# A hybrid DeltaNet/Mamba layer: the first gate blocks between the last tokens' norms, the stream's sums ahead of the taps, the second gate pair in eight products

## The chip, the cores and the metric

The kernel runs on one core of a Trainium2 chip. The metric is the device time of one execution in microseconds (us), the median of several runs. A core has TensorE (PE, matrix products), VectorE (DVE), ScalarE (ACT), GpSimd (POOL) and SyncE (SP), whose queue issues most of the transfers; each works through its own list of instructions in order and waits for the others by semaphores. Tiles lie in SBUF; products are accumulated in the banks of PSUM, 128 partitions of 512 float32 values each.

## The reference, cut to what matters

One layer over 1024 latent tokens (a grid of 16 rows of 64) with a prefix of 256 context tokens, width 1024, all float32. The token mixers (a gated DeltaNet and a Mamba-2 scan, side by side) are not touched by the change; it lies between their output and the feed-forward.

```python
mod = silu(c) @ w_ada + b_ada                       # (6 * 1024,)
sh1, sc1, g1, sh2, sc2, g2 = split(mod, 6)
...
x = x + g1 * (mix_x @ w_out)                        # 1024 x 1024
h = rmsnorm(x, norm2_g) * (1 + sc2) + sh2
a = dwconv2d_grid(h @ w_gate, conv_w, conv_b)       # 3x3 depthwise over the 16 x 64 grid
x = x + g2 * ((silu(a) * (h @ w_up)) @ w_down)      # w_gate, w_up: 1024 x 2816, w_down: 2816 x 1024
return rmsnorm(x, final_norm_g)
```

## The kernel before

**Tiling.** Tokens go in eight tiles of 128 (called tokens 0 to 7 below, `t` in the code). A float32 product is made of three matmuls in a shorter format: each operand is split into a high part (a cast, names in `h`) and a low part (what is left, names in `l`), and high by high, high by low and low by high are summed in PSUM. One matmul is 128x128 by 128x512. The 2816 columns of the feed-forward are 22 blocks of 128, taken as 11 pairs (`FORD` lists them; a pair is block j and block j + 11).

**Order.** The instructions of each engine are put in order by a scheduler of the language, which starts from the order of the code and runs its own estimate of the time; the code steers it by where a call stands, by the number of buffers of a tile, and by explicit dependences. The order shown further down is its result.

**From the output projection to the norm.** The loop over `half` and `c` makes the output projection (L1350) for four tokens and 512 columns at a time: 24 matmuls into one bank, then a multiplication by the gate row and an addition of the residual into `x1[t]`. The last round is the second half of the tokens (4 to 7) with `c` = 0. When a token has both halves of its columns, `norm2(t)` runs: a square with a sum on ScalarE, a scale and shift of that sum (L104 helper), a power on POOL (L1292), two wide operations on `u` (the second, the shift, is on POOL for tokens 0 to 3 and on VectorE from 4 on, `SHD`), eight transposes on TensorE (L1323), and out of PSUM the high part `mxh` (cast, L1325) and the low part `mxl` (L95 helper). These two hold the stream h, transposed, until the end of the feed-forward. Meanwhile the adaLN rows `aac` are summed up on POOL (L98) and spread over the partitions by TensorE (L689). `x1` goes to DRAM (`x_d`, L1327).

**First gate pair.** Only after the loop are the PSUM pools of the mixers closed and that of the feed-forward (`ps2`) opened: two images of 1024 columns (two banks each, tag `img`) and four single banks (`pb`). `first_gate` loads and splits the weights `gh`, `gl` of two blocks, and `fmm` (L1301) makes their images, 24 matmuls for each half of the tokens, 96 in all.

**Stream sums, taps, first up pair.** From the second pair on, a pair is made by a form with seven block products rather than eight (`group7`, L1459): the four weight blocks are combined by sums on POOL, the stream by sums T1 to T4 (`tq`, loop over `u`: four additions of high and low part and four subtractions on VectorE, then casts L1594 and low parts), and the products are combined by VectorE as they leave PSUM (`combine`; the first, P1, is copied by ScalarE at L1536). One product is 12 matmuls, a pair 84. `conv` takes an image: the centre tap on ScalarE writes `fac`, eight more taps on VectorE (L107) add to it, ScalarE makes the SiLU; the taps are queued in `todo` and handed out by `pop`. The up blocks of the first pair are plain products (96 matmuls, `fmm`), copied to SBUF by ScalarE and multiplied with `fac` later.

**Steady loop and end.** The products then alternate: gate pair 1, gate pair 2, up pair 1, gate pair 3, up pair 2, and so on (`seq7`; pairs count from 0). `prepare` runs four products ahead, and a pair's weights are loaded (`raw`, L1429) when its first product is prepared. Finished pairs are combined again for a seven-product form of the down projection (`asums`: stores to `sa_d`, L1509; `wsums` for `w_down`: stores to `sw_d`, L1498), which comes last (L1717), with the reload of `x1` (L1753) for the residual and the final norm.

In the names, a number behind a letter group is only the buffer's (`fac11` excepted: there it is the block).

Of the kernel before, what the change touches and what calls it, by code (L numbers as in the profile page):

```python
# [18 lines left out]
P = 128  # L19
# [54 lines left out]
def hybrid_layer(ctx: ExitStack, tc: tile.TileContext, x, c, cx, c_ctx, w_ada, b_ada, norm1_g, w_in,  # L74
# [1206 lines left out]
    rot = dict(ob="BXA")  # L1281
# [22 lines left out]
    with pool("op") as op:  # L1304
        lp["op"] = op
        for n_, shape, dt, b_ in (("n2g", [P, 512], F32, 1), ("abi", [1, 512], F32, 1), ("aac", [P, 512], F32, 2),
                                  ("awa", [P, 2, 512], F32, AWB), ("xr", [P, D], F32, XRB), ("u", [P, D], F32, 2)):
            T(op, shape, "res_" + n_, dt, tag=n_, bufs=b_)
        for j, n_ in ((2, "sc2row"), (1, "sh2row")):
            rows[j] = T(op, [P, D], n_)  # L1310
        for n_, dt, b_ in (("owr", F32, 2), ("owh", F32R, OWB), ("owl", F32R, OWB)):
            T(op, [P, 512], "res_" + n_, dt, tag=n_, bufs=b_)

        def norm2(t):
# [4 lines left out]
            for i in range(2):  # L1319
                pb = bank("ip")  # L1320
# [12 lines left out]
        for half in range(2):  # L1333
            for c in ((0, 1), (1, 0))[half]:
                if not (half and c):
                    if half + c == 0:
                        wout(0, 0, ws, KO[W0N:], (0,) * 8)
                    else:
                        ws = {}
                        wout(c, half, ws, KO, WHERE[half])  # L1340
                for t in range(4 * half, 4 * half + 4):
# [3 lines left out]
                    pb = rbank("ob")  # L1345
# [16 lines left out]
                    if c == 1 - half:  # L1362
                        norm2(t)
        rows[3] = T(tka[0], [P, D], "g2row", tag="grow")
        for b in (6, 7):
            ada_put(op, bank("tp"), b, late_ac[b])


        def first_gate(f):
            ws = []  # L1370
            for i in range(2):
                raw = T(op, [P, 512], f"gr{f}{i}", tag="owr", bufs=2)
                nc.sync.dma_start(raw.rearrange("p (k m) -> p k m", m=P),
                                  w_gate[512 * i:512 * i + 512, f * P:(f + 1) * P].rearrange("(k p) m -> p k m", p=P))
                wh = T(op, [P, 512], f"gh{f}{i}", F32R, tag="owh", bufs=OWB)
                wl = T(op, [P, 512], f"gl{f}{i}", F32R, tag="owl", bufs=OWB)
                nc.scalar.copy(wh, raw)
                tt(wl, raw, wh.bitcast(F32), ALU.subtract)
                ws.append([w.rearrange("p (k m) -> p k m", m=P) for w in (wh, wl)])
            return [lambda k, j=j: ws[k // 4][j][:, k % 4, :] for j in range(2)]  # L1380


        pspx.__exit__(None, None, None)
        ps2 = ctx.enter_context(pool("ps2", space=PSUM))

        def image():
            cnt[0] += 1
# [476 lines left out]
```

## Time and profile before

| | us |
|---|---|
| median of 3 runs | 1562.47 |
| lowest and highest | 1554.84, 1564.5 |
| the profiled execution | 1562.9 |
| its span | 1561.1 |

The profile is of one execution; its clock starts with the span. "Busy" counts work and not waiting, and a row of the timeline gives start, length, engine, line, operation, tiles (written tile, arrow, read tiles), shape and count, and in brackets how long the engine had been idle and what released it. L92, L95, L98, L104 and L107 are one-line helpers for ScalarE, VectorE and POOL operations, so the tiles' names say which of their uses a row is. The mean granted clock of TensorE in the profiled execution is 0.961 of full speed.

The page in shares of the span:

| engine | busy us | share |
|---|---|---|
| PE | 1417.2 | 91% |
| DVE | 1174.8 | 75% |
| ACT | 738.5 | 47% |
| POOL | 809.8 | 52% |

### The profile page before, as it was taken

Reading aid. Unit: us, or ns where it says so; the run is one execution under the profiler, and the core shown is the slowest. Engines: PE = TensorE matmul, PEld = TensorE weight load, DVE = VectorE, ACT = ScalarE, POOL = GpSimd, SP = SyncE. Lnnn points to the kernel's source line nnn. Section 1 sums busy time; section 2 is a strip of 40 time slices with the busy share of each in tenths; the row PEclk is TensorE's granted clock in tenths of the full one; section 3 lists DMA queues with packets and bytes.
Section 4 is the critical chain, followed back from the end, with each engine's and each line's share of the span. In section 5 each row is a group of like instructions: output and inputs, shape, how many; then the busy total and the mean of one; then the engine's idle time right before and its main releaser. Section 6 shows DMA issues by size and latency. Waiting matters only on the chain. (4 is left out here: it accounts for less than half of the span.)

```text
span 1561.1 us, 24442 instructions
## 1 busy us (share of the span) xinstructions
PE 1417.2 (91%) x8104; PEld 1172.1 (75%) x8104; DVE 1174.8 (75%) x1875; ACT 738.5 (47%) x1655; POOL 809.8 (52%) x797
## 2 busy tenths in 40 slices
PE   5899888999999889998995948999999998999997
PEld 2577776777888789997774736877787787788786
DVE  5877688977536666547987679989999999557686
ACT  6566645636666656455243243333333333365553
POOL 3554499782125775301474278687888888200001
PEclk8999999999999999999997979999999999999999
DMA  7454777654668685444962024344444444996732
GB/s 262 131 148 138 235 214 216 172 151 113 184 188 300 193 254 182 139 126 161 323 217 81 24 78 162 109 148 155 154 157 151 146 154 166 342 322 212 228 108 108
DMA packets 269308, 275.14 MB, mean 176 GB/s; under 512 B 51936, under 2 KB 194909, under 8 KB 269183
## 3 DMA queue, kind: packets, MB, share of 16 engines
q1 hardware_dynamic: 259935, 244.10, 49.6%
q0 software_dynamic: 7904, 26.74, 4.6%
q10 hardware_dynamic: 1344, 2.75, 0.5%
q8 instruction: 64, 1.05, 0.3%
q14 instruction: 61, 0.50, 0.1%
HBM read 196.06 MB, written 77.46 MB: 175 GB/s over the span
## 5 line engine op out<-in xcount | busy, mean ns | idle before, releaser
L1439 ACT CAST wh<-rw 128x512 fp32r<-128x512 f32 x282 | 165.7, 620 | 289.5 <-POOL rw L98 92.9
L98 POOL TENSOR_TENSOR wl<-rw,wh 128x512 fp32r<-128x512 f32 x144 | 199.5, 1405 | 86.5 <-ACT wh L1439 83.7
L107 DVE SCALAR_TENSOR_TENSOR fac<-im,v,fac 128x945 f32<-128x945 f32 (+2 forms) x176 | 209.6, 1209 | 29.6 <-ACT fac L92 26.8
L1459 PE MATMUL pb<-mxh,wh 128*128 128x512 f32 x320 | 128.9, 403 | 37.0 <-ACT wh L1439 17.8
L1459 PE MATMUL pb<-tq,wh 128*128 128x512 f32 x480 | 147.0, 390 | 1.8 <-ACT wh L1439 1.8
L95 DVE TENSOR_TENSOR wl<-rw,wh 128x512 fp32r<-128x512 f32 x138 | 92.1, 702 | 56.3 <-ACT wh L1439 56.2
L455 PE MATMUL bk<-hh,wh 128*128 128x512 f32 x320 | 129.6, 406 | 0.7 <-DVE v L256 0.7
L455 PE MATMUL bk<-hh,wl 128*128 128x512 f32 x320 | 129.5, 405 | 0.0
L1459 PE MATMUL pb<-mxl,wh 128*128 128x512 f32 x320 | 127.5, 398 | 1.8 <-POOL mxl L98 1.8
L455 PE MATMUL bk<-hl,wh 128*128 128x512 f32 x320 | 128.6, 402 | 0.0
L1459 PE MATMUL pb<-mxh,wl 128*128 128x512 f32 x320 | 127.0, 397 | 0.0
L98 POOL TENSOR_TENSOR rw<-rw,rw 128x512 f32<-128x512 f32 x80 | 111.5, 1406 | 13.3 <-DMA rw<-in_ffn_w_up_dram 6.4
L1787 POOL TENSOR_TENSOR ss<-ss,mhalf 128x1 f32<-128x1 f32 x8 | 7.3, 920 | 198.0 <-DVE ss L95 198.0
L1459 PEld LDWEIGHTS pb<-tq,wh 128*128 128x128 f32 x480 | 90.4, 188 | 21.5 <-ACT wh L1439 2.5
L1459 PEld LDWEIGHTS pb<-mxh,wh 128*128 128x128 f32 x320 | 61.9, 193 | 53.7 <-ACT wh L1439 18.2
L1459 PE MATMUL pb<-tq,wl 128*128 128x512 f32 x240 | 92.0, 390 | 0.7 <-POOL wl L98 0.7
L1459 PEld LDWEIGHTS pb<-mxl,wh 128*128 128x128 f32 x320 | 62.1, 194 | 14.9 <-POOL mxl L98 2.2
L1459 PEld LDWEIGHTS pb<-mxh,wl 128*128 128x128 f32 x320 | 61.8, 193 | 13.2
L455 PEld LDWEIGHTS bk<-hh,wh 128*128 128x128 f32 x320 | 61.7, 193 | 13.3 <-PE bk L254 0.9
L455 PEld LDWEIGHTS bk<-hh,wl 128*128 128x128 f32 x320 | 61.7, 193 | 13.1 <-issue 0.9
L455 PEld LDWEIGHTS bk<-hl,wh 128*128 128x128 f32 x320 | 61.7, 193 | 12.1 <-issue 0.2
L95 DVE TENSOR_TENSOR rw<-rw,rw 128x512 f32<-128x512 f32 x56 | 68.3, 1241 | 0.5 <-DMA rw<-in_ffn_w_down_dram 0.2
(415 smaller groups left out, 4160.8 us busy)
## 6 DMA issues: line engine op xcount, KB each, us to landing
rw<-in_ffn_w_down_dram SPq DMA_DIRECT2D x77, 256.0 KB
rw<-sa_d SPq DMA_DIRECT2D x77, 256.0 KB
kv<-kv_d SPq DMA_DIRECT2D x80, 192.0 KB
yq<-yq_d SPq DMA_DIRECT2D x64, 192.0 KB
awa<-in_w_ada_dram SPq DMA_DIRECT2D x24, 512.0 KB
rw<-in_ffn_w_up_dram SPq DMA_DIRECT2D x44, 256.0 KB
sa_d<-fac SPq DMA_DIRECT2D x44, 256.0 KB
sw_d<-rw SPq DMA_DIRECT2D x44, 256.0 KB
```

The lines of the kernel that those rows point to most:

```text
L95: nc.vector.tensor_tensor(o, a, b, op=op)
L98: nc.gpsimd.tensor_tensor(o, a, b, op=op)
L107: nc.vector.scalar_tensor_tensor(o, a, s, b, op0=op0, op1=op1)
L455: paced(nc.tensor.matmul(pb[:, :bn], w[i][:, kk, :], hview(h, k, b0, bn), start=(n == 0), stop=(n == 3 * KT - 1)))
L1439: nc.scalar.copy(h, r)
L1459: nc.tensor.matmul(pv, w[:, q], m[:, :, k, :], start=(n == 0), stop=(n == 11))
L1787: nc.gpsimd.tensor_tensor(rs, rs, mhalf[:, 0:1], op=ALU.pow)
```

## The change

1. The feed-forward's PSUM pool is opened before the products of the last four tokens, and these and their transposes use its four single banks. `early_gate` puts gate work between them: at token 5 the weights of the first gate pair are loaded and split, at tokens 5 and 6 the low token halves of the two images are written, at token 7 both high halves. The adaLN rows 6 and 7 go through the same banks.
2. In the feed-forward's set-up the first up block's weights are cast before the centre taps of the first pair. The stream's sums are now a function; sums 0 and 1 stand ahead of the first pair's taps (the first tap waits in VectorE's order behind their last subtraction), sums 2 and 3 behind the up products.
3. The second gate pair is made of plain products (96 matmuls) straight into its images, without weight sums and without combining. The first pair's up products are multiplied ahead of it.
4. A pair's weights are loaded seven products ahead, not four; the taps are handed out in other numbers per product; the first `wsums` comes with the first up pair of the loop.
5. `x1` is reloaded by one call for each block of the second down product, not in a loop of its own.
6. The pool of `sm` is laid before that of `fac`, `aac` moves behind `sc2row` and `sh2row`, and the banks of the output products rotate over another set.

```diff
-    rot = dict(ob="BXA")
+    rot = dict(ob="BXE")
...
+        def early_gate(t):
+
+            if t == 5:
+                first_im.extend(image() for f in FORD[:2])
+                fw0.extend(first_gate(f) for f in FORD[:2])
+            if t in (5, 6):
+                fmm(first_im[t - 5][:, LOH], *fw0[t - 5], 0)
+            if t == 7:
+                for b in range(2):
+                    fmm(first_im[b][:, HIH], *fw0[b], 512)
...
-                pb = bank("ip")
+                pb = pp["pb"]() if pp else bank("ip")
...
+                if half and not c:
+                    pspx.__exit__(None, None, None)
+                    ps2 = ctx.enter_context(pool("ps2", space=PSUM))
+                    pp["pb"] = pbank
...
-                    pb = rbank("ob")
+                    pb = pp["pb"]() if pp else rbank("ob")
...
+                    if half and not c:
+                        early_gate(t)
...
-        for i in range(2):
-            for b in range(2):
-                fmm(first_im[b][:, HB[i]], *fw0[b], 512 * i)
...
-    def conv(f, im, ac):
+    def conv(f, im, ac, behind=None):
...
+        if behind is not None:
+            tc.add_manual_dep(ctr.ins, behind.ins.name, NOSYNC, reason="first up columns first")
...
+            if behind is not None and i == 0:
+                tc.add_manual_dep(x_.ins, hist["sub"].ins.name, NOSYNC, reason="sums of the stream first")
...
+    parts = {("u", 0): [split(w) for w in wplain["u", 0]]}
+    first_cast = hist["cast"]
...
-    for u in range(4):
+    def tsums(u):
...
+    tsums(0)
+    tsums(1)
     for b in range(2):
         acs[0, b] = fac(FORD[b])
-        conv(FORD[b], im0[b], acs[0, b])
-    groups = {("g", 1): group7(w_gate, FORD[2], FORD[3])}
+        conv(FORD[b], first_im[b], acs[0, b], first_cast)
...
+    tsums(2)
+    tsums(3)
+    for b in (1, 0):
+        wplain["g", b] = wload(w_gate, FORD[2 + b])
+    for i, r in enumerate(up0):
+        o = acs[0, i // 2][:, HB[i % 2]]
+        tt(o, r, o, ALU.mult)
+    for b in (1, 0):
+        parts["g", b] = [split(w) for w in wplain["g", b]]
+        im = image()
+        plain("g", b, parts["g", b], [im[:, q] for q in HB])
+        acs[1, b] = fac(FORD[2 + b])
+        conv(FORD[2 + b], im, acs[1, b])
+    groups = {("g", 2): group7(w_gate, FORD[4], FORD[5])}
+    asums(0, acs.pop((0, 0)), acs.pop((0, 1)))
...
-    for j in range(1, NP + 1):
+    for j in range(2, NP + 1):
...
-    AHEAD = 4
+    AHEAD, LOADS7 = 4, 7
...
-        pop(2 if n in (3, 6) or j == NP - 1 else 1)
+        pop((2, 2, 2 if k == "u" else 1, 0 if k == "u" else 1, 1, 1, 1)[n])
+        if (k, j, n) == ("u", 1, 3):
+            wsums(0)
...
+            if p == "P4" and j < NLC:
+                nc.gpsimd.dma_start(x1[j], x1_d[j])
```

**The order on TensorE around the last four tokens.** Of the kernel before: the last matmul of token 7's output product (written to a bank `bk`; `owh` is the high part of `w_out`), the spreading of an adaLN row, and the transposes of `u3` to `u5`, the normalised tokens 3 to 5.

```order
L1350 MATMUL bk468_9582<-owh013_9434,mxl_8507 128x512
L689 MATMUL bk471_9631<-aac6_9103,ones_69 128x512
L1323 MATMUL bk453_9259<-ident_64,u3_9253 128x128 x4
L1323 MATMUL bk454_9266<-ident_64,u3_9253 128x128 x4
L689 MATMUL bk472_9634<-aac7_9178,ones_69 128x512
L1323 MATMUL bk460_9471<-ident_64,u4_9465 128x128 x4
L1323 MATMUL bk461_9478<-ident_64,u4_9465 128x128 x4
L1323 MATMUL bk463_9519<-ident_64,u5_9513 128x128 x4
L1323 MATMUL bk464_9526<-ident_64,u5_9513 128x128 x4
```

All four products stood ahead of the transposes of tokens 3 to 7. Of the changed kernel, the end of token 5's product (bank `pb462`), the transposes of token 5 and the start of token 6's product (`pb467`):

```order
L1394 MATMUL pb462_9490<-owh013_9434,mxh_8506 128x512
L1394 MATMUL pb462_9490<-owl013_9435,mxh_8506 128x512
L1394 MATMUL pb462_9490<-owh013_9434,mxl_8507 128x512
L1363 MATMUL pb463_9523<-ident_64,u5_9517 128x128 x4
L1363 MATMUL pb464_9530<-ident_64,u5_9517 128x128 x4
L1394 MATMUL pb467_9588<-owh010_9392,mxh_8506 128x512
L1394 MATMUL pb467_9588<-owl010_9393,mxh_8506 128x512
L1394 MATMUL pb467_9588<-owh010_9392,mxl_8507 128x512
```

Product and transposes now take turns; ahead of these rows stand token 4's product, the low halves of both images (48 matmuls) and token 4's transposes, and behind them token 6's transposes, token 7's product and transposes, and the high halves.

**The order on ScalarE behind the first images.** Of the kernel before: the centre taps (`fac` from `im`), the casts of the up weights (`wh`) and of the stream's sums (`tq`).

```order
L92 ACTIVATE fac0_9886<-im473_9641,v2_119,v3_120 128x1024
L92 ACTIVATE fac11_9888<-im474_9642,v2_119,v3_120 128x1024
L1439 CAST wh486_9815<-rw475_9786 128x512
L1439 CAST wh487_9819<-rw476_9788 128x512
L1439 CAST wh519_9961<-rw477_9790 128x512
L1439 CAST wh520_9965<-rw478_9792 128x512
L1594 CAST tq10_9782<-rw483_9802 128x512
L1594 CAST tq20_9784<-rw484_9803 128x512
```

Of the changed kernel, the same piece:

```order
L1450 CAST wh479_9794<-rw475_9786 128x512
L1450 CAST wh480_9798<-rw476_9788 128x512
L1480 ACTIVATE fac0_9844<-im465_9538,v2_119,v3_120 128x1024
L1480 ACTIVATE fac11_9846<-im466_9539,v2_119,v3_120 128x1024
L1450 CAST wh501_9911<-rw477_9790 128x512
L1450 CAST wh502_9915<-rw478_9792 128x512
L1627 CAST tq10_9782<-rw485_9810 128x512
L1627 CAST tq20_9784<-rw486_9811 128x512
```

The first up block's casts moved ahead of both centre taps; the second up block's casts and the stream's stay behind them.

**The order on SyncE at the second gate pair.** Of the kernel before: the last load of the first up pair's weights, loads of gate weights (`rw` from `in_ffn_w_gate_dram`), and the first stores of the finished first pair (`sa_d0` to `sa_d2`).

```order
L1429 DMA rw478_9792<-in_ffn_w_up_dram 128x4x128
L1429 DMA rw511_9890<-in_ffn_w_gate_dram 128x4x128
L1429 DMA rw512_9892<-in_ffn_w_gate_dram 128x4x128
L1429 DMA rw513_9894<-in_ffn_w_gate_dram 128x4x128
L1429 DMA rw514_9896<-in_ffn_w_gate_dram 128x4x128
L1509 DMA sa_d0_102<-fac0_9886 128x512
L1509 DMA sa_d1_103<-fac11_9888 128x512
L1509 DMA sa_d2_104<-fac11_9888 128x512
```

Of the changed kernel:

```order
L1440 DMA rw478_9792<-in_ffn_w_up_dram 128x4x128
L1530 DMA sa_d0_102<-fac0_9844 128x512
L1530 DMA sa_d1_103<-fac11_9846 128x512
L1530 DMA sa_d2_104<-fac11_9846 128x512
L1440 DMA rw521_10024<-in_ffn_w_gate_dram 128x4x128
L1440 DMA rw522_10026<-in_ffn_w_gate_dram 128x4x128
```

The stores of the first pair now stand ahead of the second gate pair's loads, where the loads stood ahead of the stores.

More of the change, by code (lines that the diff above doesn't have):

```diff
@@ L1418, in hybrid_layer @@
     fp = fpx.__enter__()
-    for n_, sh_, b_ in (("fac", NTL, 4), ("sm", 512, 6)):
+    for n_, sh_, b_ in (("sm", 512, 6), ("fac", NTL, 4)):
         T(fp, [P, sh_], "res_" + n_, tag=n_, bufs=b_)
@@ L1690, in hybrid_layer @@
             prepare(i + AHEAD)
+        if i + LOADS7 < len(prods) and prods[i + LOADS7][2] == 0:
+            k2, j2, _ = prods[i + LOADS7]
+            groups.setdefault((k2, j2), group7(w_gate if k2 == "g" else w_up, FORD[2 * j2], FORD[2 * j2 + 1]))
         if n == 0:
```

104 lines of the change are left out of this document (49 added, 55 removed).

## The prediction

> **What bounds the kernel now.** I read the page first (head and groups), then the share of busy time by stretches around the change, then TensorE's own timeline there, then the chain of one token's norm.
>
> ```profile
> span 1561.1 us, 24442 instructions
> L1459 PE MATMUL pb<-mxh,wh 128*128 128x512 f32 x320 | 128.9, 403 | 37.0 <-ACT wh L1439 17.8
> 836.00:853.00 17.00, 8.66 (x35) 6.52 (x36) 13.60 (x19) 7.24 (x14) 2.84 (x5) 0.60 0.29 94
> 853.00:876.00 23.00, 22.62 (x97) 18.29 (x95) 4.86 (x7) 2.14 (x3) 0.00 (x0) 0.97 0.00 1
> 876.00:902.00 26.00, 23.81 (x96) 19.09 (x96) 25.11 (x28) 7.48 (x13) 14.78 (x9) 0.93 0.14 40
> 902.00:919.00 17.00, 0.00 (x0) 0.00 (x0) 16.95 (x19) 8.96 (x15) 7.64 (x6) 0.61 0.00 0
> 1000.00:1300.00 300.00, 291.03 (x1271) 238.47 (x1270) 270.59 (x301) 104.33 (x152) 243.44 (x180) 0.99 0.48 159
> ```
>
> The stretches' columns are length, busy us of PE, PEld, DVE, ACT and POOL, granted PE clock, DMA share, GB/s. The long loop (last row) is TensorE's: 291 of 300 us. Ahead of it the bound changes hands. From 836 to 853 the norms of tokens 4 to 7 run and TensorE has half its time idle, though the output products of these tokens are long done. From 853 to 876 it works on the first gate pair while VectorE has 4.9 of 23 us of work: the taps wait for the image, and the stream's sums stand behind the first taps in VectorE's order. From 902 to 919 it is the other way round: VectorE full, TensorE empty. These 17 us are the prize; what was late there is VectorE's backlog.
>
> ```profile
> 827.77 1.09 PE L1323 MATMUL bk<-ident,u 128*128 128x128 f32 x8
> 843.05 1.07 PE L1323 MATMUL bk<-ident,u 128*128 128x128 f32 x8 [2.62 <-DVE ss L104]
> 851.13 1.94 PE L1323 MATMUL bk<-ident,u 128*128 128x128 f32 x8 [2.40 <-DVE u L95]
> 852.73 0.78 PE L1301 MATMUL im<-mxh,gh 128*128 128x512 f32 x1
> 864.12 0.39 PE L1301 MATMUL im<-mxl,gh 128*128 128x512 f32 x1
> 864.35 0.39 PE L1301 MATMUL im<-mxh,gl 128*128 128x512 f32 x1
> 875.23 0.39 PE L1301 MATMUL im<-mxh,gl 128*128 128x512 f32 x1
> 877.42 0.50 PE L1301 MATMUL pb<-mxh,wh 128*128 128x512 f32 x1 [1.80 <-ACT wh L1439]
> 879.05 0.63 PE L1301 MATMUL pb<-mxl,wh 128*128 128x512 f32 x1
> 879.48 0.63 PE L1301 MATMUL pb<-mxh,wh 128*128 128x512 f32 x1
> 900.84 0.39 PE L1301 MATMUL pb<-mxh,wl 128*128 128x512 f32 x1
> 919.03 0.80 PE L1459 MATMUL pb<-mxh,wh 128*128 128x512 f32 x1 [17.80 <-ACT wh L1439]
> 970.73 0.76 PE L1459 MATMUL pb<-mxh,wh 128*128 128x512 f32 x1 [5.66 <-DVE im L95]
> ```
>
> The reader sees the order: transposes of token 3 at 827.77, of tokens 5 and 7 at 843.05 and 851.13 with some 2.5 us of waiting each, gate from 852.73 to 875.6, up to 901.2, then the 17.80 us gap. A warm matmul comes every 0.227 us (864.35 less 864.12, and 48 of them up to 875.23), so 24 take 5.4 us and 96 take 21.8. Behind a wait of 1.80 us the spacing is 0.43 (879.48 less 879.05) for some eight matmuls, which adds 1.6 us.
>
> **The change part by part.** *Gate blocks among the norms.* In the order that TensorE now has, each of the products of tokens 5, 6 and 7 stands behind the transposes of the token ahead of it; before, all four stood ahead of them. TensorE executes the products in that order here, so each norm becomes a chain of its own with TensorE at its end:
>
> ```profile
> 794.14 0.69 DVE L95 TENSOR_TENSOR x<-bk,g1row 128x512 f32<-128x512 f32 x1 [2.81 <-PE bk L1350]
> 787.21 0.69 DVE L95 TENSOR_TENSOR x<-x,xr 128x512 f32<-128x512 f32 x1
> 844.68 1.07 ACT L92 ACTIVATE u<-x 128x1024 f32<-128x1024 f32 x1
> 845.64 0.20 ACT L92 ACTIVATION_READ_ACCUMULATOR u<-x 128x1 f32 x1
> 847.17 0.14 DVE L104 TENSOR_SCALAR ss<-ss 128x1 f32<-128x1 f32 x1
> 847.39 0.55 POOL L1292 TENSOR_TENSOR ss<-ss,mhalf 128x1 f32<-128x1 f32 x1 [3.79 <-DVE ss L104]
> 847.97 1.28 DVE L107 SCALAR_TENSOR_TENSOR u<-x,ss,sc2row 128x1024 f32<-128x1024 f32 x1 [0.66 <-POOL ss L1292]
> 849.77 1.21 DVE L95 TENSOR_TENSOR u<-u,sh2row 128x1024 f32<-128x1024 f32 x1
> 823.13 2.23 POOL L98 TENSOR_TENSOR aac<-aac,awa 128x512 f32<-128x512 f32 x1
> ```
>
> Product ready, times gate 0.69, plus residual 0.69, square and read 1.16 (844.68 to 845.84), 0.14, 0.55, 1.28, 1.21: 5.72, and seven hand-overs of about 0.12 (0.08 from the 0.14 to POOL's power, 0.15 from the last add to the transposes): 6.5 us. From the square alone to the transposes it was 6.45 in this row's run, with VectorE busy elsewhere in between, so the ends are 2.4 us (the waits seen, if most of the chain overlaps) and 8. I take 6.5, since in the new order VectorE has nothing else there. Only token 4's chain is covered, by the low halves of the gate pair (48 matmuls, 10.9 us).
>
> Walk: token 3's transposes 825.5 (one of POOL's 2.23-us adds fewer stands ahead of its shift); 1.7 for them and 5.4 + 1.6 for token 4's product: 834.2; low halves 10.9: 845.1; token 4's transposes 1.0 and token 5's product 5.4: 851.5; three waits of 6.5 (19.5), three sets of transposes at 1.6 (851.13 to 852.73) and two products at 7.0: 889.8; last cast 1.2: 891.0; high halves 10.9 + 1.6: gate pair done at 903.5 against 875.6, 27.9 us later. Ninety-six up matmuls follow at once (no 1.80 wait): 925.3 against 901.2, 24 later.
>
> The clock comes first as the rows have it: granted 0.60 in 836 to 853, where no wait was longer than 2.7 us, and 1.6 us lost behind a wait of 1.80. I therefore charge each wait with 1.6, short or long. The Trainium skill, "TensorE: Matmul & The Clock Gate", Part 1 (the clock gate), has it that only idle stretches of some 3.4 us bring half clock. By it the three waits of 6.5 would be charged the same and the sum would stay 1574, but waits of 2.4 would be free of it, and the rival with short waits would come out 3 times 1.6 lower, near 1556; the rows just named speak against that.
>
> *Sums ahead of taps, up's casts ahead of the centre taps.*
>
> ```profile
> 870.22 1.21 ACT L92 ACTIVATE fac<-im,v,v 128x1024 f32<-128x1024 f32 x1 [16.52 <-PE im L1301]
> 872.58 2.49 DVE L95 TENSOR_TENSOR rw<-mxh,mxl 128x512 f32<-128x512 f32 x4
> 871.46 1.20 DVE L107 SCALAR_TENSOR_TENSOR fac<-im,v,fac 128x945 f32<-128x945 f32 x1 [17.04 <-ACT fac L92]
> 920.74 6.83 DVE L95 TENSOR_TENSOR fac<-rw,fac 128x512 f32<-128x512 f32 x4
> 877.44 5.47 POOL L98 TENSOR_TENSOR wl<-rw,wh 128x512 fp32r<-128x512 f32 x4 [29.51 <-ACT wh L1439]
> 1133.21 3.08 DMA rw<-in_ffn_w_gate_dram
> ```
>
> VectorE can do the 16 operations of two sums (0.62 each, 10 us) from 891 to 901 under the high halves. Then it stops: the low part of the next stream block waits for ScalarE's cast, and this stands behind the second image's centre tap, which waits for 903.5. With 1.2 for it, two weight casts and two stream casts at 0.54 and two low parts, the taps run from about 909.5. Sixteen at 1.17 are 18.7; some 13 sum operations among them 8; the two products of up and gate that end the backlog, with their share of 6.83, 3.4: 939.6 us. Both sides of the bargain are in this: ten of VectorE's us are moved under TensorE's work, seven are lost behind the centre tap.
>
> *Second gate pair in eight products.* 96 matmuls for 84 adds 12, 2.7 us, and takes away POOL's four weight sums, VectorE's seven combining operations and the 5.66-us wait for the image they wrote. Its first loads now stand on SyncE's queue behind three stores of the first pair's products, which wait for 939.6. From there: 3.1 to land (1133.21 row), 0.6 cast, 1.4 low part (5.47 by 4), some 0.5 of hand-overs: 945.2. Then 96 and the next product's 12 matmuls, 24.5, and 1.6 of warm-up: the third gate pair's first product leaves PSUM at 971.3.
>
> ```profile
> 951.35 0.58 ACT L1536 COPY sm<-pb 128x512 f32<-128x512 f32 x1
> 976.63 0.56 ACT L1536 COPY sm<-pb 128x512 f32<-128x512 f32 x1
> 994.73 0.58 ACT L1536 COPY sm<-pb 128x512 f32<-128x512 f32 x1
> 1313.27 0.76 PE L1459 MATMUL pb<-mxh,wh 128*128 128x512 f32 x1 [4.55 <-DVE fac L95]
> 1342.77 4.25 POOL L1753 DMA_DIRECT2D x1r<-x_d  x8 [0.30 <-POOL rw L98]
> ```
>
> These rows are the copies of the third gate pair's first product (951.35), the second up pair's (976.63, it held the 5.66 wait) and the fourth gate pair's (994.73). Mine: 971.3 (+20), then 84 matmuls, 19.1, each: 990.4 (+13.8) and 1009.5 (+14.8).
>
> *Loads seven products ahead, other turns for taps, wsums earlier.* The steady loop has the same order on VectorE, POOL and SyncE. Its waits behind the two named are 37.0 less 17.80 less 5.66, that is 13.5 us in all, 4.55 of it at the end at 1313. I take 3 us off for a later start that lets taps and loads catch up (ends: 0 and 13.5). *Reload of x1 block by block:* in POOL's order the eight loads have no wait for a product between them, so they leave together as at 1342.77: nothing, hidden behind the down products. *Laying sm ahead of fac, other bank rotation:* nothing on the way found.
>
> Sum: +14.8 less 3, about +11.5 on the profiled execution's 1562.9 (span 1561.1 and 1.8 around it), which is level with the median 1562.47: 1574.
>
> **The rivals.**
>
> *The loop absorbs it.* For it: 13.5 us of waits stand in the loop. Against it: TensorE is busy 291 of 300, and most of these waits are handed on from VectorE's work on each pair, which does not shrink. Eight or more regained gives 1557 to 1566.
>
> *The token waits are short.* If chains of neighbours overlap to the 2.4 us seen before, the three waits cost 12.3 less; the backlog of VectorE begins as much sooner: about 1561.
>
> *Other side: the second gate pair follows up without a gap.* If, besides, the gate loads land in time (SyncE's three stores released early because the taps were done under the up products), TensorE has no wait of some 20 us at 925 (945.2 less 925.3): 1574 less 12 less 19 is 1543. It decides where the taps start before 895, that is token waits under 3 us. Against it: taps, sums and products are 30 us of VectorE work behind an image that ends after the last norm, and up is only 21.8. The Trainium skill, same page, Part 2, says that matmuls keep program order and only weight loads are pulled ahead; no later product can fill the waits by it, and no row here shows one that did.
>
> *Worse.* Chains of 8 us (VectorE, ScalarE and POOL sharing the last transposes' casts and the sums), three times 1.5, and a low part that waits on POOL behind the stream's low parts (29.51 us was such a wait's length before; some 5 here): 1583.
>
> *The change does nothing there.* For the reload this is the forecast itself.
>
> **How the numbers follow.** A measurement of this kernel tells about 1% from no change, 15.6 us: 1546.8 and 1578.1. Serial waits, 1568 to 1582 around 1574: 0.52, of it 0.12 over 1578. Absorbed: 0.15. Short waits: 0.08. No gap: 0.08. Worse: 0.17, all of it slower. Faster 0.08; slower 0.12 and 0.17, 0.29; the rest 0.63. The range 1557 to 1586 leaves out the no-gap case and about half of the worse one.
>
> **What would show it.** Right: three waits of TensorE of 5 to 8 us ahead of the transposes of tokens 5, 6 and 7; gate pair ended near 903; VectorE at 10 us of sums before its first tap and stopped near 905; a wait of some 20 us after the up pair, with gate loads landing behind the stores; third gate pair's first product near 971. Wrong: waits under 3 us, the second gate pair starting before 935, or a loop whose waits add to under 6 us. A start that is level with before and a total that is not would put the cause into the loop, against this account.

## The result and the profile after

| | median us | lowest to highest | ratio to before, 95% interval |
|---|---|---|---|
| before | 1563.49 | 1554.84 to 1565.35 | |
| changed | 1580.62 | 1578.81 to 1582.6 | 1.0121 [1.008, 1.0161] |

The change makes the kernel 1.2% slower, 17 us by the medians. The forecast was 1574, 11.5 us slower; the time lies in the range and in the upper tail of the likeliest case (1568 to 1582). By the forecast's own line of 1% it is not in the likeliest class, "within 1%" (0.63), but just over into "slower" (0.29), and the interval leaves both open. The profiled execution of the changed kernel took 1582.6 us and is thus 2 us above its median; 19.7 us lie between the two profiles.

The first two lines are the page's head and the group of TensorE's matmuls whose idle time before them was 37.0 us before:

```profile
span 1580.6 us, 24421 instructions
L1472 PE MATMUL pb<-mxh,wh 128*128 128x512 f32 x304 | 120.9, 398 | 13.0 <-DVE fac L95 12.7
```

The idle time of this group fell to 13.0, which looks like a gain; the waits have only gone to other rows. The stretches of the changed kernel show where (length, busy us of PE, PEld, DVE, ACT and POOL, granted PE clock, DMA share, GB/s):

```profile
803.00:824.00 21.00, 5.97 (x25) 5.20 (x26) 11.63 (x17) 11.41 (x21) 17.41 (x12) 0.50 0.36 117
836.00:853.00 17.00, 12.03 (x58) 9.70 (x56) 6.02 (x9) 2.23 (x4) 1.14 (x2) 0.93 0.13 52
853.00:876.00 23.00, 15.69 (x64) 13.09 (x64) 7.96 (x10) 3.50 (x6) 1.14 (x2) 0.75 0.09 34
902.00:919.00 17.00, 17.00 (x76) 14.08 (x75) 16.63 (x13) 4.28 (x8) 9.47 (x7) 1.00 0.00 0
919.00:932.00 13.00, 1.78 (x8) 1.13 (x6) 13.00 (x17) 4.09 (x5) 1.27 (x1) 0.76 0.00 0
1000.00:1300.00 300.00, 291.52 (x1271) 238.66 (x1270) 275.17 (x309) 102.80 (x150) 238.47 (x177) 0.99 0.44 147
```

Of the kernel before, the stretch that answers to the first of these:

```profile
803.00:830.00 27.00, 24.05 (x111) 18.07 (x109) 25.23 (x26) 13.10 (x23) 22.43 (x16) 1.00 0.48 165
```

The gap at 902 to 919 is filled (17.00 of 17), and a new one stands at 919 to 932. Further ahead, where TensorE had been busy for 24.05 of 27 us it is busy for 5.97 of 21, and from 853 to 876 it has 15.69 us of work instead of 22.62. The loop is what it was: 291.5 of 300. TensorE's timeline of the changed kernel has the waits one by one:

```profile
805.40 1.94 PE L1363 MATMUL bk<-ident,u 128*128 128x128 f32 x8 [7.54 <-DVE mxl L95]
814.42 1.97 PE L1363 MATMUL bk<-ident,u 128*128 128x128 f32 x8 [7.08 <-POOL u L98]
821.94 1.97 PE L1363 MATMUL bk<-ident,u 128*128 128x128 f32 x8 [5.55 <-POOL u L98]
841.53 1.03 PE L1363 MATMUL pb<-ident,u 128*128 128x128 f32 x8
854.20 1.97 PE L1363 MATMUL pb<-ident,u 128*128 128x128 f32 x8 [6.17 <-DVE u L95]
868.47 1.97 PE L1363 MATMUL pb<-ident,u 128*128 128x128 f32 x8 [6.11 <-DVE u L95]
882.46 1.97 PE L1363 MATMUL pb<-ident,u 128*128 128x128 f32 x8 [6.11 <-DVE u L95]
942.53 0.80 PE L1301 MATMUL im<-mxh,wh 128*128 128x512 f32 x1 [21.76 <-ACT wh L1450]
997.78 0.73 PE L1472 MATMUL pb<-tq,wh 128*128 128x512 f32 x2 [2.08 <-DVE im L95]
1330.57 0.77 PE L1472 MATMUL pb<-mxh,wh 128*128 128x512 f32 x1 [4.60 <-DVE fac L95]
```

Token 4's transposes (841.53) have no wait: the low halves cover its norm. Tokens 5, 6 and 7 wait 6.17, 6.11 and 6.11. The first three rows are the transposes of tokens 1, 2 and 3; the products that filled these waits before are now behind them: the first matmul of token 4's product starts at 823.56, right behind token 3's transposes. The wait of 21.76 is the one ahead of the second gate pair. What held VectorE and that pair, from the timelines of the other engines:

```profile
899.06 1.21 ACT L1480 ACTIVATE fac<-im,v,v 128x1024 f32<-128x1024 f32 x1 [3.55 <-PE im L1301]
900.16 1.13 ACT L1450 CAST wh<-rw 128x512 fp32r<-128x512 f32 x2
901.19 2.19 ACT L1627 CAST tq<-rw 128x512 fp32r<-128x512 f32 x4
902.37 1.58 DVE L95 TENSOR_TENSOR tq<-rw,tq 128x512 fp32r<-128x512 f32 x1 [6.45 <-ACT tq L1627]
903.87 3.48 DVE L95 TENSOR_TENSOR rw<-rw,rw 128x512 f32<-128x512 f32 x2
907.27 1.78 DVE L1500 TENSOR_TENSOR sm<-rw,rw 128x512 f32<-128x512 f32 x1
908.97 13.68 DVE L1490 SCALAR_TENSOR_TENSOR fac<-im,v,fac 128x945 f32<-128x945 f32 x12
935.47 1.28 DVE L95 TENSOR_TENSOR fac<-rw,fac 128x512 f32<-128x512 f32 x2
934.38 2.73 SPq L1530 DMA_DIRECT2D sa_d<-fac  x3
937.15 5.38 SPq L1440 DMA_DIRECT2D rw<-in_ffn_w_gate_dram  x8
```

ScalarE's second centre tap waits for the image, the casts stand behind it, VectorE stands 6.45 us behind the cast, and the taps begin at 908.97. The first pair's last products end at 936.75, and SyncE issues the three stores and right behind them the gate loads.

### The profile page after: what moved, and what is told of

It is laid out like the page before. It is cut to its first block, busy times and chain, and to the rows that moved or that the text cites. A ratio compares the mean times of both kernels' runs of the same rounds, so it can differ in the third digit from the quotient of the medians.

```text
span 1580.6 us, 24421 instructions
## 1 busy us (share of the span) xinstructions
PE 1421.9 (90%) x8116; PEld 1178.2 (75%) x8116; DVE 1163.4 (74%) x1868; ACT 735.1 (47%) x1651; POOL 800.7 (51%) x790
## 5 line engine op out<-in xcount | busy, mean ns | idle before, releaser
L98 POOL TENSOR_TENSOR wl<-rw,wh 128x512 fp32r<-128x512 f32 x141 | 195.4, 1402 | 80.0 <-ACT wh L1450 76.5
L1490 DVE SCALAR_TENSOR_TENSOR fac<-im,v,fac 128x945 f32<-128x945 f32 (+2 forms) x176 | 209.7, 1211 | 24.8 <-ACT fac L1480 20.8
L1472 PE MATMUL pb<-tq,wh 128*128 128x512 f32 x456 | 139.7, 391 | 2.5 <-DVE im L95 2.1
L1472 PE MATMUL pb<-mxh,wh 128*128 128x512 f32 x304 | 120.9, 398 | 13.0 <-DVE fac L95 12.7
L1472 PE MATMUL pb<-mxl,wh 128*128 128x512 f32 x304 | 119.9, 395 | 0.0
L1472 PE MATMUL pb<-mxh,wl 128*128 128x512 f32 x304 | 119.6, 393 | 0.0
L98 POOL TENSOR_TENSOR rw<-rw,rw 128x512 f32<-128x512 f32 x76 | 105.6, 1400 | 8.6 <-DMA rw<-in_ffn_w_up_dram 6.0
L1472 PEld LDWEIGHTS pb<-tq,wh 128*128 128x128 f32 x456 | 85.7, 188 | 21.3 <-DVE im L95 2.5
L1472 PE MATMUL pb<-tq,wl 128*128 128x512 f32 x228 | 87.5, 389 | 0.0
L1472 PEld LDWEIGHTS pb<-mxh,wh 128*128 128x128 f32 x304 | 57.8, 190 | 28.9 <-issue 16.1
L455 PEld LDWEIGHTS bk<-hh,wh 128*128 128x128 f32 x320 | 62.2, 195 | 13.4 <-PE bk L254 0.9
L107 DVE SCALAR_TENSOR_TENSOR rs<-up,v2h,rs 128x1281 f32<-128x1281 f32 (+1 forms) x40 | 60.6, 1515 | 9.5 <-ACT rs L92 9.3
```

The costliest lines, as they stand in the source:

```text
L98: nc.gpsimd.tensor_tensor(o, a, b, op=op)
L107: nc.vector.scalar_tensor_tensor(o, a, s, b, op0=op0, op1=op1)
L455: paced(nc.tensor.matmul(pb[:, :bn], w[i][:, kk, :], hview(h, k, b0, bn), start=(n == 0), stop=(n == 3 * KT - 1)))
L1472: nc.tensor.matmul(pv, w[:, q], m[:, :, k, :], start=(n == 0), stop=(n == 11))
L1490: x_ = nc.vector.scalar_tensor_tensor(o, iv[:, r0 + dy:r1 + dy, c0 + dx:c1 + dx], cw(i), o, ALU.mult, ALU.add)
```

## The experiments

Each run is timed beside the kernel before on the same chip. Where runs are compared, the ratios count, since the median of before was between 1559.5 and 1563.5; 0.001 is about 1.6 us. The output projection starts between 714.1 and 722.9 us in these profiles, ahead of the stages that the edits move (719.96 before, 716.63 changed), so start times of two runs compare only to within some us.

**Products ahead of the transposes.** In the last round of the loop the norm of a token is written behind the product of the next one, and the order is fixed:

```diff
+                    if t + 1 in last_mm and t >= 4 and k == 0:
+                        tc.add_manual_dep(tr.ins, last_mm[t + 1].ins.name, NOSYNC, reason="next product first")
...
-                    if c == 1 - half:
+                    if half and not c:
+                        if t > 4:
+                            norm2(t - 1)
+                        if t == 7:
+                            norm2(t)
+                        early_gate(t)
+                    elif c == 1 - half:
                         norm2(t)
-                    if half and not c:
-                        early_gate(t)
```

> The changed kernel (1580.6 us), in which each of the output products of tokens 5, 6 and 7 is issued ahead of the transposes of the token before it; nothing else is moved. Theory S (the three waits of 6.1 us behind the serial norms are what the change pays): two of the three are covered by a product each, the sum of the waits ahead of the transposes falls from 18.4 us to 8 or less, the first gate pair ends 10 to 18 us sooner, and the time is 1563 to 1571. Rival V (VectorE's backlog of sums and taps sets what follows, wherever the waits are): the waits fall, the second gate pair starts no more than 3 us sooner, 1577 to 1581.

1565.93 us, ratio 1.0043 [1.002, 1.0066]: 14.7 us below the changed kernel by the medians, 12 by the ratios. TensorE's timeline (transposes of tokens 5, 6, 7; second gate pair):

```profile
845.75 1.03 PE L1365 MATMUL pb<-ident,u 128*128 128x128 f32 x8
857.30 1.03 PE L1365 MATMUL pb<-ident,u 128*128 128x128 f32 x8
863.66 1.94 PE L1365 MATMUL pb<-ident,u 128*128 128x128 f32 x8 [5.33 <-DVE u L95]
923.54 0.79 PE L1301 MATMUL im<-mxh,wh 128*128 128x512 f32 x1 [21.77 <-ACT wh L1458]
```

One wait of 5.33 is left of three, and all that follows, the gap of 21.77 with it, moved forward by 19 us (942.53 to 923.54). Of these, 2.7 stand already at token 3's transposes (819.25 here, 821.94 there), ahead of the edit, so the edit moved it by some 16. Theory S stands: two covered waits are 13 us, and the time fell by about as much.

**The first part undone.** The gate pair and the change of PSUM's hands are put back behind the loop; with them go the banks for the output products and the adaLN rows 6 and 7. The rest stays.

```diff
-    rot = dict(ob="BXE")
+    rot = dict(ob="BXA")
...
-                if half and not c:
-                    pspx.__exit__(None, None, None)
-                    ps2 = ctx.enter_context(pool("ps2", space=PSUM))
-                    pp["pb"] = pbank
...
-                    if half and not c:
-                        early_gate(t)
...
+        pspx.__exit__(None, None, None)
+        ps2 = ctx.enter_context(pool("ps2", space=PSUM))
+        for t in (5, 6, 7):
+            early_gate(t)
```

> The changed kernel with its first part undone: the four output products stand early again, the first gate pair is made after the loop over the tokens, PSUM changes hands there. Sums, taps, second gate pair and loop stay as changed. Theory S: the first gate pair ends near 876 instead of 899, all that follows moves with it, and the time is 1554 to 1562, below the kernel before. Rival P (the other parts cost as much as the first): 1570 or more.

1557.67 us, ratio 0.9984 [0.9966, 1.0002]. The first part costs 23 us by the medians (21 by the ratios), and without it the kernel is as fast as before, perhaps slightly faster. VectorE and TensorE's second gate pair in this run:

```profile
878.45 1.58 DVE L95 TENSOR_TENSOR tq<-rw,tq 128x512 fp32r<-128x512 f32 x1 [15.48 <-ACT tq L1625]
918.62 0.79 PE L1301 MATMUL im<-mxh,wh 128*128 128x512 f32 x1 [21.75 <-ACT wh L1448]
```

With an image that comes a whole gate pair behind the norms, VectorE stands 15.48 us, not 6.45, behind the cast on ScalarE.

**The second gate pair's loads ahead of the up products.**

```diff
+    for b in (1, 0):
+        wplain["g", b] = wload(w_gate, FORD[2 + b])
     up0 = []
...
     tsums(3)
-    for b in (1, 0):
-        wplain["g", b] = wload(w_gate, FORD[2 + b])
```

> The changed kernel, in which the loads of the second gate pair's weights are issued ahead of the up products, so that they no longer stand behind the stores of the first pair. Theory L (the 21.8 us wait of TensorE ahead of the second gate pair ends with these loads): the pair can start when the first images' taps are done, near 931 instead of 942.5 us, and the time is 1569 to 1573. Rival V (the low parts on POOL and the taps on VectorE end at the same time anyway): the pair starts within 3 us of before and the time is 1577 to 1581.

1575.05 us, ratio 1.0086 [1.0061, 1.0111]: 5.5 us less than the changed kernel, between the two ranges. The intervals overlap, so the gain in time is not shown by itself; the trace shows what moved. TensorE:

```profile
930.64 0.77 PE L1301 MATMUL im<-mxh,wh 128*128 128x512 f32 x1 [8.40 <-DVE fac L1490]
1001.66 0.77 PE L1472 MATMUL pb<-mxh,wh 128*128 128x512 f32 x1 [5.90 <-DVE fac L95]
```

The wait fell from 21.76 to 8.40 and the pair starts at 930.64, as theory L had it: now it waits for the taps that still read the first images. Half of the 11.9 us came back as a wait of 5.90 for VectorE's backlog at the fourth gate pair, where the changed kernel waits for 0.41 (at 1012.28).

**Parts 3 and 4 undone.** The second pair in seven products, as before the change; early gate blocks and early sums stay.

```diff
-        plain("g", b, parts["g", b], [im[:, q] for q in HB])
...
+    groups = {("g", 1): group7(w_gate, FORD[2], FORD[3])}
...
-    for j in range(2, NP + 1):
+    for j in range(1, NP + 1):
...
-    AHEAD, LOADS7 = 4, 7
+    AHEAD, LOADS7 = 4, 4
```

> The changed kernel with its parts 3 and 4 undone: the second gate pair in seven products with weight sums on POOL and combining on VectorE, loads four products ahead, taps and wsums handed out as before; the early gate blocks and the sums ahead of the taps stay. Theory S: the front is as late as in the changed kernel, and the eight products no longer save the wait for the image, 1580 to 1590. Rival Q (the plain pair and its loads behind the stores are the cost): 1575 or less.

1601.37 us, ratio 1.0265 [1.0225, 1.0306], 20.8 us above the changed kernel and beyond theory S, which had the sign right and not the size. Rival Q falls: the plain pair pays, together with what goes with it here.

**The loads' lead alone.** `LOADS7` from 7 to 4, the pair's loads issued ahead of `prepare`.

> The changed kernel with a pair's weights loaded four products ahead, as before, instead of seven. Forecast: the loads are hidden either way, 1578 to 1583. Rival: the longer lead is what keeps the loop's waits short, 1586 or more.

1580.48 us, ratio 1.0123 [1.0093, 1.0153]: nothing, as forecast. The 20.8 us are then those of the plain pair and of the turns of taps and `wsums` that go with it.

**Part 2 alone.** Parts 3 and 4 undone as in the run of the seven products, and the first part undone as well: what is left of the change is the early casts of the first up block and the order of the sums. Three smaller things stay as well: the reload of `x1` block by block (part 5), the place of the pools of `sm` and `aac` (part 6), and the pair's loads ahead of `prepare`; no run takes them out by themselves.

> The kernel before with part 2 alone: the first up block's casts and the stream's sums 0 and 1 ahead of the first pair's centre taps and taps, sums 2 and 3 behind the up products; gate pair after the loop, second gate pair in seven products, loads four ahead. Theory A (the parts add up: with all but parts 3 and 4 the time was 1601.4, and the first part is worth 23): 1574 to 1582, slower than before by some 1%. Rival F (as forecast, VectorE's sums under the gate products are worth what the stop behind the centre tap costs): 1558 to 1566.

1575.28 us, ratio 1.0081 [1.0051, 1.011]. Theory A stands: alone, this part (with those three) costs 8 to 17 us. The first two of these lines are POOL's (the second is the first operation of the first line's five, by itself), the others are TensorE's, at the second gate pair:

```profile
911.00 14.95 POOL L98 TENSOR_TENSOR tq<-rw,tq 128x512 fp32r<-128x512 f32 x5 [11.43 <-ACT tq L1625]
911.00 10.07 POOL L98 TENSOR_TENSOR tq<-rw,tq 128x512 fp32r<-128x512 f32 x1 [11.43 <-ACT tq L1625]
920.55 0.79 PE L1470 MATMUL pb<-mxh,wh 128*128 128x512 f32 x1 [20.81 <-ACT wh L1448]
927.23 0.80 PE L1470 MATMUL pb<-mxh,wl 128*128 128x512 f32 x1 [5.45 <-POOL wl L98]
```

POOL's low parts of the stream were spread from 882 to 927 before. Now half of them, those of sums 2 and 3, come as a block from 911 to 926 behind the taps, and the weights' low parts and sums of a seven-product pair stand behind them: a wait of 20.81 and a second one of 5.45. Of the block's 14.95 us, 10.07 are its first operation, which stands while VectorE works through sums 2 and 3 and products without a break up to 919.92 (see the last section). Two waits for images that VectorE combines follow on TensorE (2.37 at 952.26, 5.66 at 978.40).

**Casts ahead of the centre taps.** On the changed kernel:

```diff
-        nc.scalar.copy(h, t)
+        hist["tcast"] = nc.scalar.copy(h, t)
...
-        conv(FORD[b], first_im[b], acs[0, b], first_cast)
+        conv(FORD[b], first_im[b], acs[0, b], hist["tcast"])
```

> The changed kernel, in which ScalarE's casts of the up weights and of the stream's sums 0 and 1 are put ahead of the two centre taps. Theory C (VectorE stands 6.5 us because its low part waits for a cast behind the second centre tap): the first tap starts near 902 instead of 909 us, what follows moves with it, 1573 to 1577. Rival N (the stop is covered by a later wait, since the pair's loads and POOL's low parts end at the same time): 1579 or more.

1573.88 us, ratio 1.0089 [1.006, 1.0118]; VectorE's first taps:

```profile
901.16 13.69 DVE L1490 SCALAR_TENSOR_TENSOR fac<-im,v,fac 128x945 f32<-128x945 f32 x12
```

They begin at 901.16, 18.1 us behind the first sum (883.11) instead of 23.3 (885.69 to 908.97). Theory C stands in the trace, with 5.2 us. The time fell by 5.0 by the ratios (6.7 by the medians), and the intervals overlap, so by itself it does not show the gain.

The same edit on the kernel with part 2 alone:

> The kernel before with part 2 alone (1575.3), and the casts of the up weights and of the stream's sums 0 and 1 put ahead of the centre taps. Theory: VectorE's 15 us stop goes and its backlog moves forward by 6 to 10 us, 1563 to 1569; the second gate pair in seven products still waits for POOL's weight sums and for its image, so it stays far above 1540.7. Rival (part 2's order was all that was wrong): 1550 or less.

1568.27 us, ratio 1.008 [1.0048, 1.0111]. The median is in the theory's range, the ratio is that of part 2 alone, so no gain is shown. VectorE's stop did fall, from 15.26 to 4.88, but TensorE's wait for POOL's low parts is 5.45 as before, and that ahead of the pair 18.11. The rival falls.

**Three edits together.** Gate pair behind the loop, loads early, casts ahead of the centre taps.

> The changed kernel with three edits together: the gate pair after the loop (alone 1557.7), the second gate pair's loads ahead of the up products (alone 5.5 us less) and the casts ahead of the centre taps. With the gate pair after the loop VectorE stood 15.5 us behind the centre taps, so theory C expects 8 to 15 us more than the sum of the first two: 1537 to 1545. Rival N: the loop is TensorE's and takes the gain back, 1549 to 1554.

1540.74 us, ratio 0.988 [0.9849, 0.9912]: faster than both kernels, 1.2% below before and 40 us below the change as made (38 by the ratios). Theory C's range holds, rival N falls. No run has the first two edits without the casts, so what each adds here is not shown.

```profile
873.62 1.37 DVE L95 TENSOR_TENSOR tq<-rw,tq 128x512 fp32r<-128x512 f32 x1 [5.72 <-ACT tq L1625]
879.94 14.82 DVE L1488 SCALAR_TENSOR_TENSOR fac<-im,v,fac 128x945 f32<-128x945 f32 x13 [2.42 <-ACT fac L1478]
972.41 0.77 PE L1470 MATMUL pb<-mxh,wh 128*128 128x512 f32 x1 [5.89 <-DVE fac L95]
```

VectorE's stop is 5.72 instead of 15.48, and TensorE's gap ahead of the second gate pair is gone; the 5.89 at 972.41 is what is left of the backlog.

**Gate blocks among the norms without serial waits.** The loads and the casts as in the three edits, the first part as changed, but with the four products in the new banks first, then the low halves, then all transposes:

```diff
+                    if 7 in last_mm and t >= 4 and k == 0:
+                        tc.add_manual_dep(tr.ins, last_mm[7].ins.name, NOSYNC, reason="products first")
...
-                    if c == 1 - half:
+                    if c == 1 - half and not half:
                         norm2(t)
-                    if half and not c:
-                        early_gate(t)
+        early_gate(5)
+        early_gate(6)
+        for t in range(4, 8):
+            norm2(t)
+        early_gate(7)
```

> Gate blocks between the norms without serial waits: the changed kernel with the loads and the casts moved (as in the three edits together, 1540.7), but with the gate pair's low halves still among the norms, behind all four output products of tokens 4 to 7 and ahead of token 4's transposes. Theory B (PSUM changes hands only behind token 3's transposes, so the 96 matmuls of the four products, 22 us, that stood in TensorE's earlier waits now come after it, and the filled gaps are worth no more than that): the gate pair ends within 4 us of the kernel with the pair after the loop, 1537 to 1545. Rival G (blocks in the gaps are a gain as soon as the norms are no longer serial): 1530 to 1535.

1553.75 us, ratio 0.9956 [0.9936, 0.9975], some 12 us above the three edits and outside both ranges. TensorE, transposes of tokens 2 and 3, the first of those of tokens 4 to 7 that waited, and the last matmul of the gate pair:

```profile
815.60 1.97 PE L1365 MATMUL bk<-ident,u 128*128 128x128 f32 x8 [7.08 <-POOL u L98]
823.13 1.97 PE L1365 MATMUL bk<-ident,u 128*128 128x128 f32 x8 [5.56 <-POOL u L98]
865.64 1.94 PE L1365 MATMUL pb<-ident,u 128*128 128x128 f32 x8 [5.18 <-DVE u L95]
883.26 0.39 PE L1301 MATMUL im<-mxh,gl 128*128 128x512 f32 x1
```

Rival G falls. Theory B was right in that the waits ahead of tokens 1 to 3 stay empty, and wrong in its price: the gate pair's last matmul starts 5.8 us later than with the three edits (877.46; 4 were allowed), and the time rose by 12, so the gate pair's end is not what counts. The last norm ends at 871 instead of 855, and VectorE's sums start there. That the products cannot start before PSUM changes hands is read from the order and the code: wherever the feed-forward's pool is opened ahead of them, they stand behind token 3's transposes, and where it is opened behind the loop, they don't. No run separates the banks from the scheduler's choice.

One table puts the kernels with a plain second pair beside the kernel before. The first column is the start of VectorE's last low part of the stream (the end of the last norm), the second the copy of the third gate pair's first product, both from each run's timeline:

| kernel | last norm | third pair | between | median | ratio |
|---|---|---|---|---|---|
| before | 853.7 | 951.4 | 97.6 | 1563.5 | 1 |
| changed | 885.1 | 971.6 | 86.5 | 1580.6 | 1.0121 |
| products ahead | 866.3 | 954.9 | 88.7 | 1565.9 | 1.0043 |
| first part undone | 852.1 | 949.0 | 96.8 | 1557.7 | 0.9984 |
| loads early | 886.5 | 960.4 | 73.9 | 1575.1 | 1.0086 |
| casts ahead | 882.5 | 962.1 | 79.6 | 1573.9 | 1.0089 |
| three edits | 855.5 | 931.1 | 75.7 | 1540.7 | 0.988 |
| blocks without waits | 871.2 | 940.8 | 69.6 | 1553.8 | 0.9956 |

The first part shortens what follows the last norm by 10 us (96.8 to 86.5), since half of the gate pair is done by then, and delays the last norm by 33 (37 counted from the start of the output projection, 720.49 and 716.63). From the third pair to the end the profiled executions took 608 to 618 us in all eight kernels, so the time is decided ahead of it but for some 10 us.

## Why the prediction was right, and where it was off

*Serial norms.* Right: three waits of 6.5 were forecast, 6.17, 6.11 and 6.11 came, and covering two of them gave 12 to 15 us. The last matmul of the up pair starts at 920.39 against 900.84, 19.6 later; counted from the start of the output projection (next paragraph) it is 22.9, beside the forecast "24 later". The rule weighed there, from the Trainium skill, "TensorE: Matmul & The Clock Gate", Part 1, was not needed: the waits were long by either reading, and the clock of 853 to 876 fell to 0.75. The rows held against that rule were in part misread. "No wait was longer than 2.7 us" in 836 to 853 overlooks the one that ends at its start, in the kernel before:

```profile
836.65 2.07 PE L689 MATMUL bk<-aac,ones 128*128 128x512 f32 x2 [7.79 <-POOL aac L98]
```

So the clock of 0.60 there is not due to short waits alone. What is left of the argument are the row behind 1.80 us and the eight transposes at 851.13: they took 1.94 us behind a wait of 2.40, where those at 843.05 took 1.07 behind 2.62. "1.6 for each wait, short or long" thus holds for the long ones and for some of the short: behind the 2.08 us at 997.78 the changed kernel's matmuls come every 0.23 us from 998.35 on.

*The start.* Token 3's transposes came at 821.94, not 825.5, and the gate pair ended near 899, where the second centre tap starts on it, not at 903.5. That is nearly all the profile's own offset; the output projection starts, before and changed, at

```profile
719.96 0.48 PE L1350 MATMUL bk<-owh,mxh 128*128 128x512 f32 x1
716.63 0.71 PE L1394 MATMUL bk<-owh,mxh 128*128 128x512 f32 x2
```

With these 3.3 us added, the two are at 825.3 and 902.4, within 1.1 us of the forecast. The walk had the products behind token 3 and so paid for them, but it didn't say that the waits ahead of tokens 1 to 3 lose their filling; 20 us of empty TensorE stand there.

*The stop behind the centre tap.* "Seven are lost" was 6.45. From the centre tap's wait to the first tap it was 10 us and not 6: three sums stood behind the stop as well and took 1.7 us each (below). The two errors cancel, which is luck, and the first tap came at 908.97 against 909.5.

*Second gate pair, and the wait behind the stores.* The pair started at 942.53 (945.2 forecast). The milestones, against those of before:

```profile
971.58 0.58 ACT L1557 COPY sm<-pb 128x512 f32<-128x512 f32 x1
992.00 0.59 ACT L1557 COPY sm<-pb 128x512 f32<-128x512 f32 x1
1012.25 0.58 ACT L1557 COPY sm<-pb 128x512 f32<-128x512 f32 x1
```

These are 20.2, 15.4 and 17.5 us later than before (3.3 more if counted from the start of the output projection); forecast were 20, 13.8 and 14.8. The first agrees by two errors again: the pair started 2.7 us sooner and took 29.1 us up to this copy, not 26.1. The second is ScalarE's: the copy stands behind a centre tap and two casts (989.87 to 992.10), while TensorE went on at 990.05 without a wait. The third is the wait of 2.08 at 997.78 and one of 0.41 at 1012.28, which the working had not: a plain pair leaves its sixteen taps for later, and six of them (990.35 to 997.12 on VectorE) stand ahead of the image that TensorE waits for.

*The step that failed* is "I take 3 us off for a later start that lets taps and loads catch up". Nothing caught up: 17.5 us at 1012 were 17.3 at 1330 (1330.57 less 1313.27). The loop's waits were not fewer: the group of matmuls whose 37.0 us the forecast took apart had 13.5 behind the two named ones before, and has 13.0 now, and the last of them, for VectorE, is 4.60 after 4.55. That VectorE's work on each pair sets them, and that they shift with it, fits this; no run isolates it. The medians differ by 17.1 us and not 11.5; of these 5.6 us this term is 3 and the milestones above 2.7, as far as two profiles that differ by 3.3 us ahead of the change can tell. The sum itself was rounded down: 14.8 less 3 is 11.8.

*What the sum hid.* It followed one path and so came out, but it gave no price for parts 2 and 3 by themselves. Part 2 was described as about even ("ten are moved, seven are lost"): alone it costs 12.6 us by its ratio. The plain pair was described by 2.7 against 5.66 us: with the turns of taps it is worth some 21 in the changed kernel and, between part 2 alone and the first part undone, 0.0097 of 1561, or 15. The traces show what it leaves out. In part 2 alone TensorE waits 5.45 us for POOL's low parts, and 2.37 and 5.66 for images that VectorE combines; with the plain pair (first part undone) 1.00 and 1.07 stand there. The forecast had named the 5.66; that part 2 piles POOL's low parts up where a seven-product pair needs POOL wasn't seen.

*The rivals.* Short token waits and the gapless pair didn't occur. The place named for the gapless case, the three stores, was right: with the loads ahead of them the gap fell by 13.4 us, and with taps that start early (three edits) it vanished. "Loop absorbs" fell. The time is nearer to "worse" (1583) than to 1574, but not by its causes: the chains cost 6.1 and not 8 us, and no wait of TensorE up to the third pair ended with a low part on POOL. (The 29.51 us that the forecast took for such a wait are POOL's own idle time ahead of a low part.)

Still open: the down projection at the end took 250.0 us from 1330.57 to the span's end, against 247.8 before, 247.9 with the three edits and 249.5 with the first part undone. Its waits are mostly for ScalarE's casts of the weights, 5.0 us in all against 2.9 before; what holds the casts was not followed, and no run was made for these 2 us. Of the eight reloads of `x1`, seven left POOL in one burst (from 1359.80 on) and the last 3.85 us behind them, nearly as forecast; no run undoes this part, so its cost is not measured.

## What to carry to other kernels

Filling an engine's gaps is worth nothing where the filling needs a resource (here PSUM's banks) whose change of hands empties earlier gaps, or stands ahead of the work that the bound engine waits for: look for the time at which that engine can start, here the end of the last norm, before the share of the filled one. When work is moved ahead of a slow engine's backlog, follow each helper's queue: one cast behind one activation that waits left VectorE idle for 15 us, though moving it alone gave some 5, not clear of the noise. And undo a change by its parts: this one was a 23 us loss, a loss of about 13 and a gain of 15 to 21, and all but the first part, with two small moves of order, gave 1.2%. The early sums are still in that best kernel; whether it would be faster without them was not tried.

## What the hardware showed that was not expected

VectorE and POOL stand in one another's way when both run operations on two tiles in SBUF (`TENSOR_TENSOR`). Of the changed kernel, operations of one shape, first apart and then together (the last three lines are single operations):

```profile
930.06 1.28 DVE L95 TENSOR_TENSOR rw<-rw,rw 128x512 f32<-128x512 f32 x2
928.64 1.27 POOL L98 TENSOR_TENSOR tq<-rw,tq 128x512 fp32r<-128x512 f32 x1 [17.18 <-ACT tq L1627]
933.51 5.58 POOL L98 TENSOR_TENSOR tq<-rw,tq 128x512 fp32r<-128x512 f32 x1 [3.60 <-ACT tq L1627]
939.05 1.72 POOL L98 TENSOR_TENSOR tq<-rw,tq 128x512 fp32r<-128x512 f32 x1
939.56 1.75 DVE L95 TENSOR_TENSOR rw<-rw,rw 128x512 f32<-128x512 f32 x1
```

Apart, VectorE takes 0.64 us for one and POOL 1.27; POOL's row at 928.64 runs beside two of VectorE's taps, which read the image from PSUM, and is not slowed by them. Together there are two pictures. While VectorE's operations follow one another without a break (from 933.66 to 937.9, 0.6 us each), one POOL operation stands for 5.58 us; in the run of part 2 alone, 10.07 us, and it ends 1.1 us behind the last of VectorE's (919.92), whereupon POOL's next ones take 1.2 each. From 939 on they take turns, about 1.7 us each on both. Which of the two comes when is not shown. The Trainium skill, "Trainium Architecture — The Big Picture", "What this means for kernel authors", says that these two share a port pair and that it is an exclusive lock; the trace agrees in that one stands while the other runs, and doesn't show by which means. Here it set the 1.7 us of the three sums ahead of the first tap, and in part 2 alone it held POOL's low parts back by some 9 us.
